# One layer of an RWKV-7 / forgetting-attention trunk: y split inside the first stage, attention with two row blocks under way, transposes of the normed rows one block later, one PSUM pool

## The chip, the cores and the metric

The kernel runs on one core of a Trainium2 chip. A core has five engines with queues of their own: TensorE (PE in the profile, its weight loads PEld) for matmuls and transposes, VectorE (DVE), ScalarE (ACT), GpSimd (POOL), and SyncE (SP), which here only issues DMAs. Matmul results land in PSUM, which has eight banks of 128 partitions by 512 float32 values; everything else lives in SBUF. The metric is the time of one execution on the device in microseconds, and lower is better.

## The reference

One layer, 512 tokens and 16 meta tokens ahead of them (T = 528), width 1024:

```python
u = rmsnorm(h, norm_mix)
proj = u @ w_in                      # 1792 + 1544 + 2048 columns
y_rw = rwkv7_branch(...)             # 8 heads of 64, delta rule, group norm, gate
y_fx = fox_branch(...)               # 8 heads of 64, causal softmax with forgetting
gates = sigmoid(proj[..., C_RW + C_FX:] + b_gate)
merged = gates[..., :1024] * (y_rw @ w_out_rw) + gates[..., 1024:] * (y_fx @ w_out_fx)
h = h + merged @ w_o
z = rmsnorm(h, norm_mlp)
h = h + square(relu(z @ w_up)) @ w_down
return h[:, 16:]
```

## The kernel before

**Precision.** Every large product is made in three passes of float32r matmuls: each operand is split in a high part (a cast on ACT) and a low part (a subtraction on DVE), and high by high, high by low and low by high are added in PSUM. `split` (L269) does this for any tile, `load_h` (L229) for half of a weight block: a DMA into `wraw` (4 buffers), the cast to `whi`, the difference to `wlo`. `load_w` (L239) loads both halves, `passes` (L273) gives the three pairs.

**The front** (L280 to L1133). After a start in an order written by hand, several Python generators ("streams") issue their instructions in turns. `Turns.run` (L164) takes the first stream, by rank, whose next step is ready by a clock that the builder keeps while it writes the program (`Clock`, L62): so the order of TensorE's instructions is fixed when the program is built (L1130), and the other engines and SP are ordered by the framework's scheduler. The streams are
- `recurrent` (L1088): the RWKV heads in four pairs, of which two make a group g. Each pair needs three blocks of the projection (`okk`, `orr`, `ov`); then come `keys`, `rows`, `scores`, the matrix `inverse` of the group, and `chain` (L984), which goes through nine chunks one after the other. `group_norm` writes `y_rw`;
- `fox_features` (L614): for each of four pairs of attention heads the blocks q, k and v, their norms and the transposes of v;
- `attention` (L678): for each pair four row blocks of 128 queries. `scored(i)` makes the logits in PSUM and the softmax in a tile `pe` (2 buffers), `turned(i)` transposes it into `pT`, `mixed` multiplies by v and copies the result to `y_fx` (L752);
- `projections` (L549): 40 blocks of `u @ w_in`, 48 matmuls of 264 columns or 24 of 512 each, taken from a list `jobs` ordered by rank and time of asking (`ask`, L519). RWKV blocks have rank 1, attention blocks 2, the 16 gate blocks 9. A job may name an event (`need`) for which the stream waits before it starts the block. As the lowest stream but one, it fills what the others leave of TensorE.

The gates go to DRAM (`gd`, L589), and their blocks are the filler when nothing else is asked for. PSUM has pool `ps`: tag `pj` with 2 banks, `ch` and `py` with one each for the chain (lent to `projections` while no chain runs), `sm` with 4 for all else.

**After the front** the pools of the front are closed and others opened over their space: `hp` (`hres`, and a tag each for `yhi`/`zhi` and `ylo`/`zlo`), `ps2` for PSUM with 4 banks `po` and 4 `pd`, and `mp`. Then:
- L1150 to L1174: `y_rw` and `y_fx` are split (L1151 to L1153: eight casts and eight subtractions), and for each of 8 blocks m of w_out two groups of 12 matmuls (L1168) are made, weighed with the gates (`gl`, loaded at L1162) and summed to `mhi`/`mlo`;
- L1186 to L1192: two blocks of w_up are loaded ahead through `wraw`; L1195 to L1200: the first half of w_o's columns; L1201 to L1204: its second half is loaded, also through `wraw`, and split;
- L1212 to L1235: per block i of 128 tokens the second half's 24 matmuls (L1217), the addition, the RMS norm (L1220 to L1230), and at once eight transposes of the normed rows (L1233), whose results are split to `zhi`/`zlo`.

**The MLP** (L1240 on) goes in four slices of 8 blocks of w_up: the up products (L1247), squared ReLU, and w_down in seven products per slice (L1365) by a scheme of Strassen's kind, whose right factors are sums of quarters of w_down (`factor_sums`, L1287; raw quarters in `traw`). In the last product of the last slice (`added(0, 1, S4, ...)`, L1418) the two results x[0] and x[1] are added to `hres` (L1382) and stored (L1386).

Of the kernel before, what the change touches and what calls it, by code (L numbers as in the profile page):

```python
# [29 lines left out]
FIRST = (0, 4, 8, 12)  # L30

# [155 lines left out]
def kernel(ctx, tc, ht, x, win, par, cst, gain, lora, wout, wo, wup, wdn, out, dbg=None):  # L187
# [40 lines left out]

    def load_h(src, low, tag, bufs):  # L229
# [5 lines left out]
        A.copy(hi, raw)  # L235
        low.tensor_tensor(lo, raw, hi.bitcast(F32), ALU.subtract)  # L236
        return hi, lo
# [38 lines left out]
    yp = ctx.enter_context(tc.tile_pool(name="yp", bufs=1))  # L276
    gates_d = [dr.tile([128, S], F32, name=f"gd{i}") for i in range(16)]
    quarters = [[wdn[i][256 * c:256 * c + 256] for c in range(8)] for i in range(4)]

    with ExitStack() as st:  # L280
        up = st.enter_context(tc.tile_pool(name="up", bufs=1))
        ps = st.enter_context(tc.tile_pool(name="ps", bufs=2, space=PSUM))
# [33 lines left out]
        fF = rp.tile([8, T], F32, name="fF", tag="Bm", bufs=2)  # L316
        fF_d = dr.tile([8, T], F32, name="fF_d")
        f0 = rp.tile([8, T], F32, name="f0", tag="L0", bufs=2)
        f1 = rp.tile([8, T], F32, name="f1", tag="L1", bufs=2)
# [197 lines left out]
        asked = [0]  # L517

        def ask(rank, blk, begin, parts=((0, HT), (HT, T)), need=None):  # L519

            ev = Event()
            jobs.append((rank, asked[0], blk, begin, parts, ev, need))
            jobs.sort(key=lambda j: j[:2])
            asked[0] += 1
            return ev
# [72 lines left out]

        forgot = Event()
# [13 lines left out]

        def fox_features():  # L614
            for p in range(4):
                b0 = B_PAIR + 6 * p
                if p > 1:
                    yield fox_near[p - 2]

                def ask_normed(blk, parts, name, need=None):  # L620
                    d = {}

                    def begin():
                        c0 = parts[0][0]
                        d["f"] = f = fp.tile([128, T - c0], F32, name=name, bufs=2)
                        d["sq"] = sq = fp.tile([128, T], F32, name="fsq", tag="fsq", bufs=2)

                        def evac(po, sl):
                            d["s"] = act(sq[:, sl], po, AF.Square)
                            A.copy(f[:, sl.start - c0:sl.stop - c0], po)  # L630
                        return evac
                    d["in"] = ask(2, blk, begin, parts, need)
                    return d

                def normed(d, parts, gcol):
                    yield d["in"]
                    f, sq = d["f"], d["sq"]
                    yield lambda: max(ck.ready(sq), banks(len(parts)))
                    pin = None
                    for a0, a1 in parts:  # L640
                        pq = psm("pssq")[:, :a1 - a0]
                        mm(pq, ones_blk, sq[:, a0:a1], start=True, stop=True)
                        pin = pin or pinned(d["s"])
                        after(act(sq[:, a0:a1], pq, AF.Ln, bias=eps, scale=1.0 / 64), pin)
                    c0 = parts[0][0]
                    act(sq[:, c0:], sq[:, c0:], AF.Exp, scale=-0.5)
                    V.scalar_tensor_tensor(f, f, gcol, sq[:, c0:], ALU.mult, ALU.mult)
                    return f

                whole = ((0, HT), (HT, T))  # L650
                dq, dk, d = ask_normed(b0, SEQ, "qa", fox_done[p - 2] if p > 1 else None), ask_normed(b0 + 1, whole, "ka"), {}
                q_done = Event()

                def begin():
                    d["v"] = fp.tile([128, T], F32, name="vf", tag="fsq", bufs=2)
                    return lambda po, sl: A.copy(d["v"][:, sl], po)
                v_in = ask(2, b0 + 2, begin, need=q_done)
                q = yield from normed(dq, SEQ, qg8)
                q_done.done = True
                k = yield from normed(dk, whole, pr[:, C_KG:C_KG + 1])  # L660
                yield v_in
                vf = d["v"]
                yield lambda: max(ck.ready(vf), banks(2))
# [3 lines left out]
                for j in range(4):  # L667
                    nc.tensor.transpose(pv[:, 128 * j:128 * j + 128], vf[:, NM + 128 * j:NM + 128 * j + 128], ident)
                A.copy(vt.rearrange("p a b -> p (a b)"), pv)
                pvm = psm("pvm")  # L670
                nc.tensor.transpose(pvm[:16, :128], vf[:, :NM], ident)
                for e, hs in enumerate(hss):
                    A.copy(vm[32 * e:32 * e + 16, hs], pvm[:16, hs])
                yield forgot
# [3 lines left out]
        def attention():  # L678
            for p in range(4):
# [12 lines left out]
                def scored(i):  # L692
# [11 lines left out]
                    for e in range(2):  # L704
                        pe = fp.tile([128, T], F32, name="pe", bufs=2)
# [35 lines left out]
                def mixed():  # L741
# [52 lines left out]
        class Pair:  # L794
# [70 lines left out]
            def rows(self):  # L865

                kkn, r3, P = v9(self.okk), v9(self.orr), self.P
                self.L = l0, l1 = [rp.tile([128, NCH, 128], F32, name=f"L{e}", bufs=2) for e in range(2)]
# [17 lines left out]
            def scores(self):  # L886
# [3 lines left out]
                self.bkT = bkT = rp.tile([128, NCH, 128], F32, name="bkT", bufs=2)  # L890
                self.Bm = Bm = rp.tile([128, NCH, 128], F32, name="Bm", bufs=2)
# [92 lines left out]
        def chain(g, prs):  # L984
# [21 lines left out]
            for c in range(NCH):  # L1006
# [78 lines left out]
        values_read = [Event() for g in range(2)]  # L1085
        chained = [Event() for g in range(2)]

        def recurrent():  # L1088
# [4 lines left out]
            for g in range(2):  # L1093
                prs = pairs[2 * g:2 * g + 2]
                for j, q in enumerate(prs):
# [14 lines left out]
                    if j == 0:  # L1110
                        yield from prs[1].decay()
                    yield q.v_in
# [6 lines left out]
                if g == 0:  # L1119
                    pairs[2].ask_values(values_read[0])  # L1120
# [5 lines left out]
        turns.add(3, fox_features())  # L1126
        turns.add(8, projections(24 + 16))
# [10 lines left out]
    yhi = hp.tile([128, KB, S], F32R, name="yhi", tag="zhi")  # L1138
    ylo = hp.tile([128, KB, S], F32R, name="ylo", tag="zlo")
    ps = ctx.enter_context(tc.tile_pool(name="ps2", bufs=4, space=PSUM))  # L1140

    def ppo():
        return ps.tile([128, 512], F32, name="po")

    def ppd():
        return ps.tile([128, 512], F32, name="pd")

    with ExitStack() as st:
        mp = st.enter_context(tc.tile_pool(name="mp", bufs=1))
        ahead = [load_w(wout[0])]  # L1150
        for j, src in enumerate((y_rw, y_fx)):  # L1151
            for k in range(4):
                split(yhi[:, 4 * j + k, :], ylo[:, 4 * j + k, :], src[:, k, :])  # L1153
# [3 lines left out]
        for m in range(KB):  # L1157
            w = ahead.pop() if ahead else load_w(wout[m])
            pp = []
            for br in range(2):  # L1160
# [5 lines left out]
                for k in range(4 * br, 4 * br + 4):  # L1166
                    for a, b in passes(wk(w, k), (yhi, ylo)):
                        mm(po, a, b[:, k, :], start=n == 0, stop=n == 11)  # L1168
# [13 lines left out]
        zhi = hp.tile([128, KB, S], F32R, name="zhi", tag="zhi")  # L1182
# [313 lines left out]
```

## Time and profile before

| | us |
|---|---|
| three timed executions | 845.28, 847.02, 847.98 (median 847.02) |
| the profiled execution | 845.82 |
| its span in the trace | 844.1 |
| PE busy | 827.1 (98% of the span) |
| DVE busy | 606.7 (72%) |
| ACT busy | 453.5 (54%) |
| last matmul of the front starts | 415.21 |
| first product of w_out starts (L1168) | 417.17 |
| first up product starts (L1247) | 510.29 |
| last matmul starts | 839.73 |

The granted clock of TensorE is 1.00 in every slice. "Busy" of PE counts from the start of a matmul to its modelled end, and neighbours overlap, so 98% does not say that no time is lost: the distance from one matmul's start to the next one's does.

### The profile page before, as it was taken

The numbers are of one execution on the slowest core, as the hardware profiler recorded it, in microseconds if no ns is written. First come the engines' busy times: TensorE is split into PE (matmuls) and PEld (weight loads), VectorE is DVE, ScalarE is ACT, GpSimd is POOL, SyncE is SP. The second block draws the span as 40 slices with busy tenths as digits, with TensorE's granted clock in tenths as the row PEclk, the third lists the DMA queues.
The fourth block names the chain that finished last, engine by engine and source line by source line (L and its number), as shares of the span: only waits on it lengthen the run. The fifth ranks groups of instructions, "written<-read, shape, count | busy, mean of one in ns | idle before, by whom it ended". The sixth has DMA issues, their size and how long they took to land.

```text
span 844.1 us, 15258 instructions
## 1 busy us (share of the span) xinstructions
PE 827.1 (98%) x5746; PEld 677.1 (80%) x5746; DVE 606.7 (72%) x1208; ACT 453.5 (54%) x934; POOL 112.6 (13%) x121
## 2 busy tenths in 40 slices
PE   8989998999999999999999999999999999999998
PEld 6979886788978767877688779888888888888886
DVE  6797975679799357655556564876687777768688
ACT  7767537765763456544556442664354445544452
POOL 1011000001010000000022002204700550055000
PEclk9999999999999999999999999999999999999999
DMA  7221231101222322233486423642753374345431
GB/s 233 73 94 59 69 97 62 56 27 52 63 64 69 97 79 73 64 92 104 147 270 224 150 75 88 202 149 67 235 150 99 97 239 129 84 138 192 119 90 75
DMA packets 51338, 95.88 MB, mean 114 GB/s; under 512 B 5816, under 2 KB 6968, under 8 KB 51264
## 3 DMA queue, kind: packets, MB, share of 16 engines
q1 hardware_dynamic: 47680, 86.52, 32.8%
q0 software_dynamic: 1280, 4.20, 1.7%
q10 hardware_dynamic: 2304, 4.20, 1.5%
q8 instruction: 45, 0.74, 0.4%
q14 instruction: 29, 0.24, 0.1%
HBM read 88.57 MB, written 6.31 MB: 112 GB/s over the span
## 4 chain that ended last, share of the span: by engine, by line
PE 78%; DVE 9%; ACT 5%; DMA 4%; issue 3%; POOL 1%; SPq 0%; DVEq 0%; ACTq 0%; POOLq 0%
PE pj L575 22%; PE po L1247 21%; PE po L1365 12%; PE pd L1365 5%; DMA gl<-gd 2%; PE pw L951 2%; PE po L1217 2%; PE psc L701 2%; PE pj L390 1%; PE ppt L733 1%; DVE wlo L545 1%; DMA wraw<-in_wup 1%; PE py L749 1%; DVE wlo L236 1%; DMA wraw<-in_wo 1%
## 5 line engine op out<-in xcount | busy, mean ns | idle before, releaser
L575 PE MATMUL pj<-uhi,whi 128*128 128x264 f32 (+1 forms) x480 | 166.2, 346 | 0.0
L575 PE MATMUL pj<-ulo,whi 128*128 128x264 f32 (+1 forms) x480 | 154.0, 321 | 0.0
L575 PE MATMUL pj<-uhi,wlo 128*128 128x264 f32 (+1 forms) x480 | 154.0, 321 | 0.0
L575 PEld LDWEIGHTS pj<-uhi,whi 128*128 128x128 f32 x480 | 90.2, 188 | 14.1 <-issue 5.7
L575 PEld LDWEIGHTS pj<-ulo,whi 128*128 128x128 f32 x480 | 90.4, 188 | 6.9 <-issue 2.1
L575 PEld LDWEIGHTS pj<-uhi,wlo 128*128 128x128 f32 x480 | 90.3, 188 | 7.0
L1247 PE MATMUL po<-zhi,whi 128*128 128x512 f32 (+1 forms) x248 | 94.8, 382 | 0.0
L1247 PE MATMUL po<-zlo,whi 128*128 128x512 f32 (+1 forms) x248 | 94.8, 382 | 0.0
L1247 PE MATMUL po<-zhi,wlo 128*128 128x512 f32 (+1 forms) x248 | 94.8, 382 | 0.0
L236 DVE TENSOR_TENSOR wlo<-wraw,whi 128x512 fp32r<-128x512 f32 x84 | 65.1, 785 | 41.1 <-ACT whi L235 41.1
L235 ACT CAST whi<-wraw 128x512 fp32r<-128x512 f32 x84 | 51.3, 617 | 46.8 <-DMA wraw<-in_wup 25.2
L544 ACT CAST whi<-wraw 128x512 fp32r<-128x512 f32 x78 | 47.8, 618 | 47.8 <-PE pj L575 47.5
L545 DVE TENSOR_TENSOR wlo<-wraw,whi 128x512 fp32r<-128x512 f32 x78 | 53.0, 689 | 24.9 <-ACT whi L544 23.1
L270 ACT CAST whi<-t 128x512 fp32r<-128x512 f32 x64 | 39.9, 624 | 44.5 <-DVE wlo L271 20.6
L271 DVE TENSOR_TENSOR wlo<-t,whi 128x512 fp32r<-128x512 f32 x64 | 49.3, 784 | 18.9 <-ACT whi L270 18.0
L1365 PE MATMUL po<-wlo,fhi 128*128 128x512 f32 x160 | 62.7, 392 | 0.2 <-DVE wlo L271 0.2
L1365 PE MATMUL po<-whi,flo 128*128 128x512 f32 x160 | 62.3, 390 | 0.0
L1365 PE MATMUL po<-whi,fhi 128*128 128x512 f32 x160 | 62.0, 389 | 0.0
L1293 POOL TENSOR_TENSOR t<-traw 128x512 f32<-128x512 f32 x24 | 35.7, 1492 | 153.2 <-DVE wlo L271 134.3
L1247 PEld LDWEIGHTS po<-zhi,wlo 128*128 128x128 f32 x248 | 46.6, 188 | 9.1
L1247 PEld LDWEIGHTS po<-zlo,whi 128*128 128x128 f32 x248 | 46.6, 188 | 9.0
L1247 PEld LDWEIGHTS po<-zhi,whi 128*128 128x128 f32 x248 | 46.6, 188 | 9.0
(316 smaller groups left out, 1733.1 us busy)
## 6 DMA issues: line engine op xcount, KB each, us to landing
wraw<-in_win SPq DMA_DIRECT2D x84, 256.0 KB, 2.6
wraw<-in_wup SPq DMA_DIRECT2D x64, 256.0 KB, 3.3
wraw<-in_wdn SPq DMA_DIRECT2D x48, 256.0 KB, 2.6
traw<-in_wdn SPq DMA_DIRECT2D x48, 256.0 KB, 2.9
gd<-gt ACTq DMA_DIRECT2D x16, 256.0 KB, 2.3
wraw<-in_wout SPq DMA_DIRECT2D x16, 256.0 KB, 3.1
gl<-gd SPq DMA_DIRECT2D x16, 256.0 KB, 3.5
wraw<-in_wo SPq DMA_DIRECT2D x16, 256.0 KB, 3.3
```

Of the source, the lines that this page charges most:

```text
L235: A.copy(hi, raw)
L236: low.tensor_tensor(lo, raw, hi.bitcast(F32), ALU.subtract)
L270: A.copy(hi, x)
L271: V.tensor_tensor(lo, x, hi.bitcast(F32), ALU.subtract)
L544: after(A.copy(hi, raw), last["ACT"])
L545: after(V.tensor_tensor(lo, raw, hi.bitcast(F32), ALU.subtract), last["DVE"])
L575: mm(po, a, b[:, k, a0:a1], start=n == 0, stop=n == 23)
L701: mm(sc, q[hs, 128 * i:128 * i + 128], k[hs, a:b], start=True, stop=True)
L951: mm(ps_[hs, n - b0, :], lhs(n)[hs], rhs(n)[hs], start=True, stop=True)
L1247: mm(po[:, t0:t1], a, b[:, k, t0:t1], start=n == 0, stop=n == 23)
L1293: eng.tensor_tensor(t, sums[c, pair] if c in (T1, T2) else c, d, ALU.add)
L1365: mm(x[i], a[:, k, left, 128 * i:128 * i + 128], c, start=start and k == 0 and n == 0, stop=stop and k == n_pairs - 1 and n == 2)
```

## The change

- A pool `kp` and the PSUM pool `ps` are opened ahead of the front and live to the end. The tags L0, L1, bkT and Bm (two buffers each) of the recurrence move from `rp` to `kp`; `ppo` takes banks of tag `sm`, `ppd` those of `pj`, `ch`, `py` in turn.
- The split of y becomes a stream of the front, `divided`, of rank 4. It writes eight tiles `ys` into the slots of L0, L1, bkT and Bm, once chain 1 has ended; the last attention pair is split straight from PSUM.
- `fox_features` asks for q and k of pair 1 at the beginning, right behind pair 0's blocks, with `need` on pair 0's k and v.
- `attention` issues `scored(i + 1)` ahead of `turned(i)`; the tile `pe` has two tags by parity of the block, with two buffers each.
- The values of pair 2 of the recurrence are asked for in chain 0's last chunk but one, where before they were asked for with `need` on that place.
- The early blocks of w_up and the second half of w_o are loaded into space of `zlo` and `zhi` in place of `wraw`.
- The transposes of block i of the normed rows are called after the norm of block i + 1.
- In the last product, x[1] is made as two results of 256 columns; each is added and stored by itself, the first of the two through ACT's queue.
- The sums of w_down's quarters lie in the slots of `kp`, the raw quarters' loads on SP are kept behind the last `load_h` issued, and the scratch for dynamic DMAs is halved.

The core of the diff (of the class Fox, only what differs from the functions before):

```diff
+SLOTS = ("L0", "L1", "bkT", "Bm")
@@ load_h
-        nc.sync.dma_start(raw, src)
+        asked.append(nc.sync.dma_start(raw, src))
@@
+    kp = ctx.enter_context(tc.tile_pool(name="kp", bufs=1))
+    ps = ctx.enter_context(tc.tile_pool(name="ps", bufs=2, space=PSUM))
+        def two(j, k):
+            ys[4 * j + k] = t = kp.tile([128, 2, S], F32R, name="ys", tag=SLOTS[(4 * j + k) // 2], bufs=2)
+            return t[:, 0, :], t[:, 1, :]
+        def divided():
+            yield chained[1]
+            for k in range(2):
+                split(*two(0, k), y_rw[:, k, :])
+            for k in range(3):
+                yield fox_done[k]
+                split(*two(1, k), y_fx[:, k, :])
+            yield normalised[1][1]
+            for k in range(2, 4):
+                split(*two(0, k), y_rw[:, k, :])
@@ fox_features
+            fox = [Fox(p) for p in range(4)]
+            fox[0].ask()
+            fox[0].ask_values()
+            fox[1].ask(fox[0].k_done, fox[0].v_done)
+            for p, x in enumerate(fox):
                 if p > 1:
                     yield fox_near[p - 2]
+                    x.ask(fox_done[p - 2])
+                if p > 0:
+                    x.ask_values()
...
@@ attention
-                        pe = fp.tile([128, T], F32, name="pe", bufs=2)
+                        pe = fp.tile([128, T if i % 2 else T - 128], F32, name=f"pe{i % 2}", bufs=2)
-                    A.copy(y_fx[:, p, :], py)
+                    if p < 3:
+                        A.copy(y_fx[:, p, :], py)
+                    else:
+                        yield chained[1]
+                        split(*two(1, 3), py)
                 for i in range(4):
+                    if i < 3:
+                        nxt = yield from scored(i + 1)
+                        fox_near[p].done = i == 2
                     yield from turned(i, pes)
-                    if i < 3:
-                        pes = yield from scored(i + 1)
-                        fox_near[p].done = i == 2
+                    pes = nxt
@@ chain, recurrent
                         values_read[g].done = True
+                        if g == 0:
+                            seconds[0].ask_values()
-                    pairs[2].ask_values(values_read[0])
+                    seconds.append(pairs[2])
@@ after the front
-        for j, src in enumerate((y_rw, y_fx)):
-            for k in range(4):
-                split(yhi[:, 4 * j + k, :], ylo[:, 4 * j + k, :], src[:, k, :])
-                    for a, b in passes(wk(w, k), (yhi, ylo)):
-                        mm(po, a, b[:, k, :], start=n == 0, stop=n == 11)
+                    for a, b in passes(wk(w, k), (0, 1)):
+                        mm(po, a, ys[k][:, b, :], start=n == 0, stop=n == 11)
+        raws = [hp.tile([128, KB, S], F32, name=name + "raw", tag=name) for name in ("zhi", "zlo")]
-                raw = wp.tile([128, 512], F32, name="wraw", bufs=4)
+                raw = raws[1][:, 2 * j + x, :]
-            raw = wp.tile([128, 512], F32, name="wraw", bufs=4)
+            raw = raws[0][:, k, :]
...
-                pt = ppd().rearrange("p (b c) -> p b c", c=128)
-                for k in range(4):
-                    nc.tensor.transpose(pt[:, k, :], xt[:, 512 * j + 128 * k:512 * j + 128 * k + 128], ident)
-                A.copy(zhi[:, kk, tk], pt)
-                V.tensor_tensor(zlo[:, kk, tk], pt, zhi[:, kk, tk].bitcast(F32), ALU.subtract)
+            if normed:
+                turned(*normed.pop())
+            normed.append((i, xt))
+        turned(*normed.pop())
@@ MLP
+            if name == "traw" and queue is nc.sync:
+                after(d, asked[-1])
+            return [(0, WHOLE)] + ([(1, WHOLE)] if len(x) == 2 else [(1, cols) for cols in HALVES])
-                x = [ppo() for i in range(2)]
+                x = [ppo() for i in range(2 + end)]
+                    if end:
+                        store(a, b, i, cols, nc.scalar if n == 1 else nc.sync)
@@ kernel
-    nc = bacc.Bacc("TRN2", target_bir_lowering=False, num_devices=1, dynamic_dma_scratch_size=8192)
+    nc = bacc.Bacc("TRN2", target_bir_lowering=False, num_devices=1, dynamic_dma_scratch_size=4096)
```

More of the change, by code (lines that the diff above doesn't have):

```diff
@@ L281 @@
         up = st.enter_context(tc.tile_pool(name="up", bufs=1))
-        ps = st.enter_context(tc.tile_pool(name="ps", bufs=2, space=PSUM))
         def ppj(tag):
@@ L635, in normed @@
[L635 to L663, printed above, removed]
+                    x.ask(fox_done[p - 2])
+                if p > 0:
+                    x.ask_values()
+                q = yield from x.normed(x.dq, SEQ, qg8)
+                x.q_done.done = True
+                k = yield from x.normed(x.dk, x.WHOLE, pr[:, C_KG:C_KG + 1])
@@ L664, in fox_features @@
+                x.k_done.done = True
+                yield x.v_in
+                yield lambda: max(ck.ready(x.v), banks(2))
                 vt = fp.tile([128, 4, 128], F32, name="vt", bufs=2)
```

139 lines of the change are left out of this document (92 added, 47 removed).

## The prediction

> **What bounds the kernel now.** I read the page first, then what PE waited for, then the chain of waits in order of time, then a table by stage.
>
> ```profile
> span 844.1 us, 15258 instructions
> PE 827.1 (98%) x5746; PEld 677.1 (80%) x5746; DVE 606.7 (72%) x1208; ACT 453.5 (54%) x934; POOL 112.6 (13%) x121
> ```
> ```profile
> PE pvt L997 <- ACT gt L588: 2.1, 1, 2.1
> PE psr L898 <- DVE Bm L899: 1.9, 4, 0.8
> PE po L1168 <- ACT yhi L270: 1.6, 1, 1.6
> ...
> PE pd L1233 <- DVE xt L1230: 0.8, 1, 0.8
> ```
> ```profile
> core 0: us, PE busy (x) PEld busy (x) DVE busy (x) ACT busy (x) POOL busy (x), PEclk, DMA share, GB/s
> ...
> 352.00:415.60 63.60, 63.60 (x352) 47.26 (x351) 33.91 (x97) 28.29 (x72) 0.00 (x0) 1.00 0.30 95
> 415.60:418.00 2.40, 0.60 (x3) 0.29 (x2) 1.54 (x3) 2.40 (x5) 0.00 (x0) 1.00 0.38 106
> ...
> 515.00:844.00 329.00, 324.96 (x1484) 270.01 (x1482) 247.19 (x342) 154.46 (x245) 80.36 (x64) 1.00 0.45 138
> ```
>
> TensorE bounds every stage. In the waits' list (total, times, longest) no entry is over 2.1 us, and in the table (length of the stretch, then busy time by engine) only the handover at 415.6 to 418 is mostly empty. The change removes no matmul, so it can gain only what TensorE loses between matmuls: waits, and the switches between its kinds of work. For these I need the steady distance of starts:
>
> ```profile
> 92.30 5.82 PE pj L575 x48
> ...
> 146.75 0.92 PE pj L575 x6
> ...
> 594.22 43.52 PE po L1247 x192
> ```
>
> These are rows of the chain (start, length, what, count). A product of 512 columns takes 43.52 / 192 = 0.227 us, one of 264 columns 5.82 / 48 = 0.121. Six of the latter between other work take 0.92 and not 6 x 0.121 = 0.73: an interruption of the filler costs 0.19.
>
> **Term 1, the handover: -2.2.** The filler's last matmul, the casts of y and the first two products of w_out:
>
> ```profile
> 415.21 0.40 PE L575 MATMUL pj<-uhi,wlo 128*128 128x512 f32 x1
> ...
> 416.51 0.61 ACT L270 CAST yhi<-y_rw 128x512 fp32r<-128x512 f32 x1
> ...
> 417.17 0.49 PE L1168 MATMUL po<-yhi,whi 128*128 128x512 f32 x1 [1.57 <-ACT yhi L270]
> ...
> 417.90 0.50 PE L1168 MATMUL po<-ylo,whi 128*128 128x512 f32 x1 [0.23 <-DVE ylo L271]
> ```
>
> From 415.21 to 417.90 are 2.69 us for two steps worth 0.45, so 2.24 are lost. yhi needs the space that the filler still reads, hence the late cast. In the change the pieces of y lie in other slots and are split earlier, after chain 1; ACT is busy 28.29 and DVE 33.91 of the 63.6 us there, so eight casts of 0.61 and their subtractions fit beside the filler. Only the last attention pair can be late, and its part is wanted after 12 products of the other branch, 2.7 us. Bounds: nothing to -2.24; I take it whole, since PE's other operands, the first weights, are already in.
>
> **Term 2, the weights of w_o: -1.2.**
>
> ```profile
> 477.67 0.62 ACT L270 CAST wohi<-wraw 128x512 fp32r<-128x512 f32 x1 [2.36 <-DMA wraw<-in_wo]
> ...
> ```
> ```profile
> 478.08 0.39 PE L1200 MATMUL po<-whi,mlo 128*128 128x512 f32 x1
> ...
> 480.01 0.40 PE L1200 MATMUL po<-whi,mlo 128*128 128x512 f32 x1
> ```
>
> Three steps take 1.93 us instead of 0.68: 1.25 lost. ACT sits in order behind a cast whose load came late, since both halves of w_o share the four `wraw` buffers. With loads into the space of zlo and zhi that cast's data comes sooner. Bounds 0 to -1.25.
>
> **Term 3, the transposes: -1.2.**
>
> ```profile
> 492.54 0.39 PE L1217 MATMUL po<-wohi,mhi 128*128 128x512 f32 x1
> 493.71 0.66 PE L1233 MATMUL pd<-cs,xt 128*128 128x128 f32 x4 [0.78 <-DVE xt L1230]
> ...
> 495.11 0.39 PE L1217 MATMUL po<-wohi,mhi 128*128 128x512 f32 x1
> ```
> ```profile
> 499.90 0.39 PE L1217 MATMUL po<-wohi,mhi 128*128 128x512 f32 x1
> ...
> 501.64 0.39 PE L1217 MATMUL po<-wohi,mhi 128*128 128x512 f32 x1
> ```
>
> The same work (a product, four transposes, a product, four transposes, a product) takes 2.57 us in block 0 and 1.74 in block 1, so block 0 loses 0.83 to the norm. A block later every row is ready: this goes. The eight transposes then stand together, which saves one interruption per block, at most 4 x 0.19 = 0.76; I take 0.4. Bounds 0 to -1.6. Block 3's transposes still wait for their norm, but behind them lie the first up products, as now.
>
> **Term 4, the tail: +0.1.**
>
> ```profile
> 839.47 1.39 DVE L1382 TENSOR_TENSOR hres<-hres,po 128x512 f32<-128x512 f32 x2 [0.34 <-PE po L1365]
> ...
> 839.73 0.40 PE L1365 MATMUL po<-whi,flo 128*128 128x512 f32 x1
> ```
> ```profile
> L1081 DVE TENSOR_TENSOR y_rw<-yT,pg 128x256 f32<-128x256 f32 x8 | 3.3, 417 | 0.3
> ```
>
> The two last additions already run back to back on DVE, 0.69 each, and the last matmul ends before the second begins. Halving x[1] makes that 0.69 + 2 x 0.42 = 1.53 instead of 1.39, by the nearest row of 256 columns; 12 products become 24 halves, about the same array time. Against it the last store is half as large:
>
> ```profile
> L1386 SPq DMA_DIRECT2D out<-hres x8: 332/332/344, 814.4 to 840.9; - x8
> ...
> DMA to landing us min/median/max: 2.0/2.0/2.0
> ```
>
> Between nothing and half of 2.0 could be saved. I take 0.1 lost, bounds +0.2 and -0.9. [...]
>
> **Term 5, the front's order: -1.5.** Nothing is added or taken from TensorE there. With pair 1 asked for at the beginning its q and k stand where three gate blocks stood, and these gates fill later. `scored(i + 1)` ahead of `turned(i)` gives every attention step more time for its softmax, and pair 1 then runs beside chain 0. Each pair has 11 steps, 44 in all; where a step falls next to one of the chain's, one interruption of 0.19 goes. I take 8 of 44, an estimate: -1.5. From both sides: 20 steps more merged, -3.8; as many split apart, +3.8. One wait can go or stay:
>
> ```profile
> 134.78 0.70 ACT L588 ACTIVATE gt<-pj,pr 128x512 f32<-128x512 f32 x1
> ...
> 135.53 0.41 PE L997 MATMUL pvt<-cs,ov 128*64 128x128 f32 x2 [2.11 <-ACT gt L588]
> ```
>
> Chain 0 wants the bank `py` that a gate block borrowed, and ACT empties it late. Another block may stand there with the same effect, so I count 0, and -2.1 in the range. The later asking for pair 2's values moves a block that no one waits for now. The added `need` can hold only the `projections` stream, and pair 1's blocks stand behind pair 0's in its list anyway, so I cost it at nothing.
>
> The rest costs nothing: raw quarters, kept behind loads already issued, are wanted an up phase later, and from 515 on PE is busy 324.96 of 329 us, with no wait in the list above 0.3. The PSUM tags of `ppo` and `ppd` make again four and four banks.
>
> **The sum**: -2.2 - 1.2 - 1.2 + 0.1 - 1.5 = -6.0 us. The profiled execution took 845.82 (1.7 around its span), so 839.8. It lies 1.2 below the median of the timed runs, 847.02; from the middle of the two, 846.4, I get **840.4**.
>
> **Rivals.**
> *The handover's gain is given back (842.6).* The loads of w_up and w_o, 12 x 256 KB, can now start at 415.
>
> ```profile
> 417.00:455.00 38.00, 37.60 (x165) 30.92 (x166) 25.03 (x40) 24.15 (x43) 7.76 (x6) 1.00 0.78 258
> ```
> ```profile
> 427.32 0.60 ACT L235 CAST whi<-wraw 128x512 fp32r<-128x512 f32 x1
> ```
>
> The DMA engines are busy at 0.78 there, and 3 MB at 258 GB/s are 12 us of their work. The cast at 427.32 is that of block 2's second half, wanted by matmul 60 of the stage, at 417.90 + 59 x 0.227 = 431.3, or 429.1 if the stage starts 2.2 earlier; with its subtraction about 1 us is left. A load later by over 1 us stalls PE. For it: ACT's casts stand in order behind the gates' tanh, which wait for DMAs. Against: SP spreads such loads in time even now. Price: 2.2.
>
> *The front loses what the rest gains (844.9).* More attention beside the chains means more changes of shape on TensorE: 24 more interruptions cost 4.5. [...]
>
> *Slower (849.5 or more): the filler runs out.* The chain shows the last attention pair at
>
> ```profile
> 387.52 0.87 PE psc L701 x4
> ...
> 399.24 1.09 PE psc L701 x8
> ...
> 411.40 1.00 PE py L746 x4
> ```
>
> that is 12 us per row block, nearly all of it filled by gate blocks. If the gates were used up before the last pair's third row block, PE would stand in two such blocks with some 2 us of work in each: up to 20 us. From 8.5 us on, less than half of that, the kernel is slower. Against it: pair 1's blocks push gates back, so three more are left then, not fewer.
>
> *Some edits do nothing (842)*: the scheduler orders all but the front by readiness, so the regrouping and the loads may come out as now; that is inside the forecast's own range.
>
> **Chances.** Forecast (837 to 842.5): 0.56. A front that gains 3 us more (below 837): 0.11. Handover given back: 0.11. Front loses: 0.14. Slower: 0.08. A change of 0.3%, 2.5 us, is about what a measurement of this kernel can tell from none. The first three are faster: 0.78; the fourth counts as the same: 0.14; slower 0.08. The range takes in the front's bounds and the first two rivals, and most of the third: 835.5 to 845.
>
> **What would show it.** Right: the first L1168 starts within 0.3 us of the last filler matmul's turn; no wait of L1200 on ACT; L1233 in groups of eight; the last store no sooner after the last matmul than now; fewer runs of L575 in the front. Wrong: waits at L1168 for `whi`; attention's steps with nothing of L575 between them and PE idle; new waits of the chain's first lines.

## The result, and the profile after

The changed kernel took 841.21 us (median of 4 runs, 840.85 to 841.58) where the kernel before, timed beside it, took 847.50 (4 runs, 845.28 to 848.49): a ratio of 0.9929, 95% interval 0.9908 to 0.9950. The forecast was 840.4. The profiled execution took 840.95, with a span of 839.2, 4.9 less than before; so the sum of the prediction, -6.0 on one profiled execution, came out as -4.9, and several of its parts came out otherwise than forecast.

The page of the changed kernel begins:

```profile
span 839.2 us, 15281 instructions
PE 826.2 (98%) x5758; PEld 679.4 (81%) x5758; DVE 606.9 (72%) x1209; ACT 451.9 (54%) x933; POOL 117.8 (14%) x121
```

TensorE still bounds the kernel, and its busy time hardly moved (827.1 before, 826.2 now). The span fell by 4.9: what went was time between matmuls. Where, is read from the starts of the first matmul of each stage in the timelines (us; the last column is the span):

| | last of the filler | 1st of w_out | 1st of w_o | w_o, 2nd half | 1st up product | span |
|---|---|---|---|---|---|---|
| before | 415.21 | 417.17 | 461.31 | 484.38 | 510.29 | 844.1 |
| changed | 412.92 | 413.15 | 457.03 | 481.13 | 505.49 | 839.2 |
| difference | -2.29 | -4.02 | -4.28 | -3.25 | -4.80 | -4.9 |

By stage: the front -2.29, the handover with the second product -2.2, the rest of w_out +0.2, the first half of w_o **+1.03**, the second half with the transposes -1.55, the MLP and the tail -0.1. Four stages gained; w_out and the first half of w_o gave 1.3 us back. The two ends of that are in the timeline of TensorE in the changed kernel (start, length, line, what, and in brackets the wait in front of it):

```profile
412.92 0.39 PE L580 MATMUL pj<-uhi,wlo 128*128 128x512 f32 x1
413.15 0.62 PE L1213 MATMUL po<-ys,whi 128*128 128x512 f32 x2
...
458.62 0.50 PE L1244 MATMUL po<-whi,mhi 128*128 128x512 f32 x1 [0.75 <-DVE gl L1215]
...
467.62 0.50 PE L1244 MATMUL po<-wlo,mhi 128*128 128x512 f32 x1 [0.76 <-DVE wlo L239]
```

The first product of w_out follows the last of the filler after 0.23 us, the steady distance: the handover is gone. But the first half of w_o, where the change was to take a stall away, has two new ones. The chain of waits in front of the second says what it is (start, length, what):

```profile
459.57 5.57 DMA zhiraw<-in_wo
...
465.16 0.02 ACT wohi L273
...
465.69 0.61 ACT whi L238
466.30 0.53 ACT wohi L273
...
466.89 0.69 DVE wlo L239
```

A raw block of the second half of w_o (`zhiraw`) lands at 465.14, 5.57 us after its issue. ACT stands in order with its cast (`wohi`), and behind that stands the cast of the first half (`whi`) that TensorE needs now; the load of that one had landed at 464.51, 1.2 us before its cast began. It is the old stall of 478 again, with the same cause, sooner. The queue that issues the loads shows why (SP's own rows: start, time from the first issue to the last, what, how many):

```profile
455.19 0.33 SPq L1207 DMA_DIRECT2D gl<-gd  x1
455.57 0.42 SPq L1247 DMA_DIRECT2D zhiraw<-in_wo  x1
456.40 0.33 SPq L235 DMA_DIRECT2D wraw<-in_wo  x1
456.78 0.90 SPq L1247 DMA_DIRECT2D zhiraw<-in_wo  x2
459.20 0.33 SPq L235 DMA_DIRECT2D wraw<-in_wo  x1
459.57 0.91 SPq L1247 DMA_DIRECT2D zhiraw<-in_wo  x2
```

With room of their own, the loads of the second half no longer wait for one of four buffers, so they go out between those of the first half and of the gates (`gl`), over 20 us before anyone wants them.

### The profile page after: what moved, and what is told of

The parts are those of the page before. It is cut to its first block, busy times and chain, and to the rows that moved or that the text cites. A ratio compares the mean times of both kernels' runs of the same rounds, so it can differ in the third digit from the quotient of the medians.

```text
span 839.2 us, 15281 instructions
## 1 busy us (share of the span) xinstructions
PE 826.2 (98%) x5758; PEld 679.4 (81%) x5758; DVE 606.9 (72%) x1209; ACT 451.9 (54%) x933; POOL 117.8 (14%) x121
## 4 chain that ended last, share of the span: by engine, by line
PE 84%; DVE 6%; ACT 4%; DMA 3%; issue 2%; POOL 1%; SPq 0%; DVEq 0%; ACTq 0%; POOLq 0%
PE pj L580 24%; PE po L1302 21%; PE po L1429 12%; PE pd L1429 5%; PE po L1274 3%; PE pw L993 2%; PE psc L738 1%; PE pj L395 1%; DMA gl<-gd 1%; PE py L786 1%; PE ppt L770 1%; PE pch L1059 1%; PE po L1244 1%; PE pd L1244 1%; DVE wlo L550 1%
## 5 line engine op out<-in xcount | busy, mean ns | idle before, releaser
L239 DVE TENSOR_TENSOR wlo<-wraw,whi 128x512 fp32r<-128x512 f32 x84 | 78.6, 947 | 40.2 <-ACT whi L238 40.0
L550 DVE TENSOR_TENSOR wlo<-wraw,whi 128x512 fp32r<-128x512 f32 x78 | 52.7, 685 | 21.8 <-ACT whi L549 19.2
L1429 PE MATMUL po<-wlo,fhi 128*128 128x512 f32 (+1 forms) x164 | 63.4, 387 | 0.1
L1429 PE MATMUL po<-whi,flo 128*128 128x512 f32 (+1 forms) x164 | 62.9, 384 | 0.0
L1429 PE MATMUL po<-whi,fhi 128*128 128x512 f32 (+1 forms) x164 | 62.3, 384 | 0.0
L274 DVE TENSOR_TENSOR wlo<-t,whi 128x512 fp32r<-128x512 f32 x64 | 43.6, 689 | 24.3 <-ACT whi L273 24.1
L1318 ACT CAST fhi<-R 128x768 fp32r<-128x768 f32 (+1 forms) x32 | 30.2, 944 | 46.1 <-DVE R L1325 25.1
```

Of the source, the lines that this page charges most:

```text
L274: V.tensor_tensor(lo, x, hi.bitcast(F32), ALU.subtract)
L550: after(V.tensor_tensor(lo, raw, hi.bitcast(F32), ALU.subtract), last["DVE"])
L1318: A.copy(fhi[:, j, a:b], R[:, a:b])
L1429: mm(x[i][:, cols], a[:, k, left, 128 * rows:128 * rows + 128], c[:, cols], start=start and k == 0 and n == 0, stop=stop and k == n_pairs ...
```

## The experiments

All times are medians of 4 to 8 runs timed beside the kernel before, whose own medians were 846.6 to 847.1 in the sets of runs 1 to 12. Medians less than about 1 us apart can't be told apart where the runs behind them overlap; there the traces are compared. The last column is the stretch from the first product of w_out to the first of the second half of w_o; its 288 products need 288 x 0.227 = 65.4 us.

| | run | us | ratio to before (95%) | 1st of w_out | that stretch |
|---|---|---|---|---|---|
| | before | 847.5 | | 417.17 | 67.2 |
| | changed | 841.21 | 0.9929 (0.9908 to 0.9950) | 413.15 | 68.0 |
| 1 | front undone | 842.63 | 0.9959 (0.9947 to 0.9970) | 417.09 | 65.4 |
| 2 | raws undone | 841.89 | 0.9946 (0.9934 to 0.9958) | 413.25 | 70.1 |
| 3 | raws and handover undone | 841.73 | 0.9951 (0.9936 to 0.9965) | 414.80 | 66.8 |
| 4 | transposes undone | 841.72 | 0.9950 (0.9937 to 0.9962) | 412.69 | 68.1 |
| 5 | x and gain later | 841.87 | 0.9946 (0.9933 to 0.9958) | 412.51 | 70.6 |
| 6 | second half of w_o later | 838.72 | 0.9909 (0.9896 to 0.9923) | 412.73 | 65.8 |
| 7 | 5 and 6 | 838.93 | 0.9906 (0.9891 to 0.9921) | 413.14 | 67.1 |
| 8 | the kernel before, again | 846.01 | 0.9997 (0.9986 to 1.0009) | 416.61 | 67.5 |
| 9 | 6, handover undone | 841.04 | 0.9924 (0.9904 to 0.9943) | 415.18 | 66.4 |
| 10 | 6, attention's order undone | 835.95 | 0.9863 (0.9845 to 0.9882) | 410.35 | 66.4 |
| 11 | 6, early asking undone | 842.08 | 0.9938 (0.9920 to 0.9955) | 413.36 | 68.9 |
| 12 | 6, tail undone | 839.37 | 0.9902 (0.9883 to 0.9921) | 413.26 | 66.1 |

(In run 1 one product of w_out starts at 413.35, between steps of attention; 417.09 is the second.)

### Run 1: the front as before

```diff
-            fox[1].ask(fox[0].k_done, fox[0].v_done)
+                if p == 1:
+                    x.ask()
-                    if i < 3:
-                        nxt = yield from scored(i + 1)
...
-                    yield from turned(i, pes)
-                    pes = nxt
+                    yield from turned(i, pes)
+                    if i < 3:
+                        pes = yield from scored(i + 1)
```

> The changed kernel with attention as before: pair 1's q and k asked for behind pair 0, and `turned(i)` ahead of `scored(i + 1)`. Only the asking for pair 2's values stays changed. Theory (the order of the front ends it 2.3 us sooner, 412.92 against 415.21, by fewer interruptions of the filler and by the wait of pvt that is gone): the last filler matmul starts at 415 +- 0.5, the filler has over 100 runs where the changed kernel has 87, and the time is 841.2 + 2.3 = 843.5. Rival (it is the later asking for pair 2's values that moved the gate block out of chain 0's way): the wait of pvt stays gone and only the interruptions come back, 842.2 or less.

Measured: 842.63. The longest wait of the kernel before, of `pvt` on a gate's evacuation, is back in the list (total, times, longest):

```profile
PE pvt L1039 <- ACT gt L593: 2.1, 1, 2.1
```

The filler has 95 runs (stretches of its matmuls without others between) up to its end, not the over 100 of the theory, against 88 in the changed kernel. But the front ends in a way that neither theory named (TensorE's timeline):

```profile
410.76 0.39 PE L580 MATMUL pj<-uhi,wlo 128*128 128x512 f32 x1
410.99 0.27 PE L769 MATMUL ppm<-cs,pe 128*16 128x128 f32 x1
...
413.35 0.50 PE L1213 MATMUL po<-ys,whi 128*128 128x512 f32 x1
413.79 1.07 PE L784 MATMUL py<-pTm,vm 16*64 16x512 f32 x2
414.78 2.38 PE L787 MATMUL py<-pT,vt 128*64 128x512 f32 x16
417.09 0.50 PE L1213 MATMUL po<-ys,whi 128*128 128x512 f32 x1
```

The filler runs out at 410.76, and the last attention pair stands nearly alone until 417. So the order of the front is worth 3.7 to 3.9 us at the start of w_out (417.09 against 413.15). That the filler runs out isn't what costs them: TensorE is busy 6.21 of the 6.33 us from 410.76 on. About half of the 3.7 are waits (from 23 us to the end of the front they add up to 6.8 us, in the changed kernel to 4.9, the wait of `pvt` among them); the rest is spread over the front. Only 1.4 reach the total: with the later start the first half of w_o has no stall at all.

### Runs 2 and 3: the raw weights, and the handover with them

Run 2 loads through `wraw` again (`raw = wp.tile([128, 512], F32, name="wraw", bufs=4)` in both places). Run 3 does that, drops `divided`, and splits y behind the front into the space of `zhi` and `zlo`, as before.

> The changed kernel with the early blocks of w_up and the second half of w_o loaded through the four `wraw` buffers, as before. Theory (the loads into the space of zhi and zlo have no brake: 3 MB more are under way before 465 us, and gate and weight loads land late, which makes the two new stalls of 0.9 and 1.0 us in the first half of w_o): the stalls at 457 and 466 go, the old one of 1.25 us in front of the last steps of that half comes back, and the time is 841.2 - 1.9 + 1.2 = 840.5. Rival 1 (the prediction: the old stall comes back and nothing goes): 842.4. Rival 2 (the stalls come from the sooner start of the stage as such): the two stalls stay and the old one is back too, 842.4 as well, but with three stalls in the trace.

> The changed kernel with y split behind the front, into the space of zhi and zlo, and with all raw weights loaded through `wraw`, as before. Theory (the handover is worth 2.2 us and little of it is given back): 2.2 us above the run in which only the raws are undone, so 843 to 844, with PE waiting at the first product of w_out for yhi. Rival (handover's gain given back by loads that land late in the first half of w_o): the stalls of 0.9 and 1.0 us there shrink by as much as the handover takes, and the time is within 0.7 us of that run's.

Run 2: 841.89, from 840.38 to 843.19. Of the three cases none holds whole, though its one run at full clock took 840.38, near the theory's 840.5. The two new stalls go, as the theory had it; the old one comes back, larger, and costs more than its own length (timeline of run 2, then stretches of it, where the columns are the busy times of TensorE, its loads, DVE, ACT and POOL, the granted clock, the DMA engines' share and GB/s):

```profile
474.41 0.39 PE L1243 MATMUL po<-whi,mlo 128*128 128x512 f32 x1
476.31 0.50 PE L1243 MATMUL po<-whi,mhi 128*128 128x512 f32 x1 [1.51 <-ACT whi L238]
477.11 0.50 PE L1243 MATMUL po<-wlo,mhi 128*128 128x512 f32 x1 [0.30 <-DVE wlo L239]
```
```profile
477.00:478.00 1.00, 0.89 (x4) 0.75 (x5) 0.76 (x3) 0.89 (x2) 0.00 (x0) 1.00 0.43 121
478.00:479.00 1.00, 1.00 (x4) 0.80 (x3) 0.63 (x1) 0.00 (x0) 0.00 (x0) 0.50 0.89 334
...
481.00:482.00 1.00, 1.00 (x5) 0.80 (x4) 0.69 (x1) 0.41 (x1) 0.00 (x0) 0.79 0.62 184
```

Behind the wait TensorE is granted half its clock from 478 to about 481.4. Run 3 starts w_out 1.55 us later than run 2 and is no slower (841.73): its stretch to the second half is 66.8 us where run 2 needs 70.1, of which the half clock is 1.6. By the medians and these two traces the theory is out and the rival holds: as the loads stand here, a later handover only takes the stall out of w_o. At full clock it may be otherwise: run 2's only such run took 840.38, run 3's three 841.31 to 842.62, too few to settle it. The second half starts at 481.13 in the changed kernel, 481.60 in run 3, 482.52 in run 1, although w_out starts 4 us apart.

### Run 4: the transposes at once

The body of `turned` stands again inside the loop over j, right behind each half's norm.

> The changed kernel with each block's normed rows transposed right after their norm, as before. Theory (the norm of the first block made TensorE wait 0.8 us and the transposes in two groups of four cost one interruption more per block): PE waits for xt again, the second half of w_o is 1.2 to 1.6 us longer, and the time is 842.4 to 842.8. Rival (with the loads landing otherwise the norm is no longer late): within 0.5 us of 841.2.

Measured: 841.72, 0.5 above the changed kernel, within what the runs spread. The trace is clearer. The chain of waits shows the transposes of the changed kernel in groups of eight, and those of run 4 in fours with a product between:

```profile
492.18 0.87 PE pd L1264 x8
493.05 5.46 PE po L1274 x24
498.51 0.87 PE pd L1264 x8
```
```profile
495.89 0.60 PE pd L1290 x4
496.49 0.24 PE po L1274
496.73 0.44 PE pd L1290 x4
```

From the second half of w_o to the first up product it takes 25.16 us (480.75 to 505.91), the changed kernel 24.36, the kernel before 25.91. No wait for `xt` shows. So the regrouping is worth 0.8, more than the 0.4 assumed, and the norm's wait of 0.8 went with the other parts of the change; which of them took it away isn't shown.

### Runs 5, 6 and 7: which loads are in the way

```diff
5 -        nc.sync.dma_start(gB, gain.to_broadcast([128, 1024]))
5 +        after(nc.sync.dma_start(gB, gain.to_broadcast([128, 1024])), gls[-1])
5 -            nc.sync.dma_start(hres[:, i, :], x[128 * i:128 * i + 128, :])
5 +            after(nc.sync.dma_start(hres[:, i, :], x[128 * i:128 * i + 128, :]), gls[-1])
6 -            nc.sync.dma_start(raw, wo[1, k // 2][:, 512 * (k % 2):512 * (k % 2) + 512])
6 +            after(nc.sync.dma_start(raw, wo[1, k // 2][:, 512 * (k % 2):512 * (k % 2) + 512]), asked[-1])
```

`gls[-1]` is the last load of a gate, `asked[-1]` at that place the last load of w_o's first half; `after` only sets the order on SP's queue. Run 7 has both.

> The changed kernel with the five loads of x and gain (2.5 MB, wanted from 481 us on) held behind the last load of the gates on SP's queue. Theory (from 413 us on the DMA engines are the limit, 0.85 busy up to 457, so loads that no one needs yet push back the gates and the first half of w_o, and that is what the two new stalls of 0.9 and 1.0 us are): the stall on the gates at 457 goes, the one at 467 shrinks or goes, and the time is 839.2 to 840.3. Rival 1 (the gates' loads are late because each has only two buffers, not because of the traffic): both stalls stay, 841.2. Rival 2 (the loads of x then come too late for the additions behind the first half): the second half of w_o waits at its first additions, 842 or more.

> The changed kernel with the raw second half of w_o held on SP's queue behind the last load of its first half. Theory (the eight loads of 256 KB into the space of zhi stand between those of the first half, and ACT stands in order behind a cast whose load has not landed): the stall at 467 (1.0 us with its gap) goes, the one on the gates at 457 may stay, and the time is 840.2 to 840.7. Rival 1 (the traffic as a whole is the limit, so the order of these loads is nothing): 841.2. Rival 2 (held back, they are late for the second half, as in the kernel before): a stall near 479 to 482 of over 1 us, and 842 or more.

> Both of the former together. Theory: both stalls go, w_out and the first half of w_o take 65.5 us where the changed kernel takes 68.0, and the time is 839.0 to 839.6. Rival (11 MB are wanted between 413 and 481 whatever their order, so one stall only moves to the second half): 840.5 or more.

Run 5: 841.87. The theory falls: a wait on a gate moves into w_out (0.5), and one of 1.7 for `whi` appears at 467, again followed by a granted clock of 0.50 (the mean of this trace is 0.998). The five loads now stood right ahead of the first half's weights, and three of these took 7.6 to 7.9 us from issue to landing. In run 5 and run 7 the longest waits between 405 and 515 were

```profile
PE po L1245 <- ACT whi L238: 1.7, 1, 1.7
```
```profile
PE po L1214 <- DVE gl L1216: 1.5, 1, 1.5
```

Run 6: **838.72**, better than its theory, since both stalls went, and no run of it is as long as any of the changed kernel's (838.33 to 840.43 against 840.85 to 841.58). SP and TensorE in run 6 read

```profile
453.59 0.33 SPq L1207 DMA_DIRECT2D gl<-gd  x1
454.79 6.93 SPq L235 DMA_DIRECT2D wraw<-in_wo  x4
461.77 4.11 SPq L1247 DMA_DIRECT2D zhiraw<-in_wo  x8
```
```profile
PE po L1244 <- DVE wlo L239: 0.2, 1, 0.2
```

The last gate's load goes out 1.6 us sooner (453.59 for 455.19), the eight raw blocks follow the first half's, and of the waits between 405 and 515 one of 0.2 is left. The DMA engines are about as busy (the last two numbers are their share and GB/s):

```profile
413.00:457.00 44.00, 44.00 (x196) 36.43 (x195) 26.04 (x39) 24.69 (x42) 10.06 (x7) 1.00 0.80 271
457.00:481.00 24.00, 23.81 (x106) 19.38 (x104) 16.92 (x31) 15.64 (x30) 1.60 (x1) 1.00 0.59 191
```

In the changed kernel the same stretches show 0.85 and 0.52. So it isn't the amount of traffic but its order: loads that aren't wanted yet ahead of those that are, on one queue, and casts in that order on ACT. Run 7: 838.93, as run 6; holding x and gain back too gives nothing. Its time is about what its theory said, its stretch isn't: the wait of 1.5 us on a gate stands in w_out, and the stretch is 67.1 us, not 65.5.

### Run 8: the kernel before, once more

> The kernel before, for another trace of it: of its 11 runs on this chip nine had a mean granted clock of 0.997 or 0.998 and took 846.3 to 847.8, two had 1.000 and 0.998 and took 845.3 to 845.5, while the profile shown of it had 1.000. Theory (the stall of 2.24 us at the handover is sometimes followed by some microseconds at half the clock, as the stall of 1.9 us at 474 is in the run with the raws undone, where the clock is 0.50 from 478 to 481): the trace shows a stretch at about 0.5 behind 417 or behind another of the kernel's longest waits, and the time is 846.3 to 847.8. Rival (the clock is a little lower all over): no stretch stands out.

Measured: a median of 846.01, and 845.33 in the profiled execution, under the theory's 846.3 to 847.8 but with the stretch that it wanted (timeline, then the clock):

```profile
414.64 0.40 PE L575 MATMUL pj<-uhi,wlo 128*128 128x512 f32 x1
416.61 0.51 PE L1168 MATMUL po<-yhi,whi 128*128 128x512 f32 x1 [1.57 <-ACT yhi L270]
417.34 0.56 PE L1168 MATMUL po<-ylo,whi 128*128 128x512 f32 x1 [0.22 <-DVE ylo L271]
...
420.68 0.58 PE L1168 MATMUL po<-yhi,whi 128*128 128x512 f32 x1
421.10 0.40 PE L1168 MATMUL po<-ylo,whi 128*128 128x512 f32 x1
```
```profile
418.00:419.00 1.00, 1.00 (x4) 0.71 (x4) 1.00 (x2) 1.00 (x3) 0.00 (x0) 0.50 1.03 399
...
421.00:422.00 1.00, 1.00 (x5) 0.77 (x5) 0.49 (x1) 0.47 (x1) 0.00 (x0) 0.96 0.51 168
```

The same wait as in the first trace of this kernel is followed here by eight products 0.43 us apart (421.10 less 420.68) and not 0.227: 1.6 us, and w_out takes 45.8 us where it took 44.1. At the end of w_o's first half next to nothing of it is left (second half at 484.15, in the first trace 484.38, where the front ended 0.6 later), since the stall of 478 is gone in turn. Of the 43 timed runs of this kernel beside these experiments, this one's own among them, the six with a mean clock of 1.000 took 845.07 to 845.53; the nineteen of 0.998, this trace's value, took 845.02 to 847.84; the two of 0.999 took 846.04 and 846.36, those of 0.996 and 0.997 846.4 to 848.5, and one of 0.994 took 850.95. The changed kernel's four runs had 0.999 or 1.000. The medians of this kernel are thus 1.3 to 2.2 us above its runs at full clock (846.6 to 847.5 against about 845.3). That the long wait brings this difference too, and the change takes it away with the wait, is likely but not shown: none of the runs of 846 us or more has a trace, and the one stretch that was traced cost the total nothing. The two profiled executions of the kernels before and changed, both at 1.000, differ by 4.9.

### Runs 9 to 12: the parts again, with the loads in order

> The run with the second half of w_o held back (838.7) with one thing undone: the eight casts of y stand on ACT behind the last gate's evacuation, so behind the filler. Theory (the handover is worth the 2.2 us of the prediction, and only the disordered loads of w_o took it back): PE waits some 2 us for ys at the first product of w_out, no other stall gets shorter, and the time is 840.9. Rival 1 (the first half of w_o ends when its weights are in, whatever came before): 839.2 or less, with the first half of w_o ending at 478 to 479 as without the edit. Rival 2 (the long wait also brings the half clock, as in the second trace of the kernel before, where 410 to 430 lost 1.6 us so): 842.5, with a granted clock under 0.95 behind 415.

Run 9 sets the casts of y behind the last gate's evacuation on ACT (`after(A.copy(hi, src[:, k, :]), gated[-1])`). Measured: 841.04, the theory's 840.9:

```profile
413.22 0.39 PE L580 MATMUL pj<-uhi,wlo 128*128 128x512 f32 x1
415.18 0.50 PE L1215 MATMUL po<-ys,whi 128*128 128x512 f32 x1 [1.57 <-ACT ys L1199]
415.91 0.50 PE L1215 MATMUL po<-ys,whi 128*128 128x512 f32 x1 [0.23 <-DVE ys L1200]
```

From the filler's last matmul to the second product are 2.69 us, to the hundredth as in the kernel before, and the total is 2.3 above run 6. (In the traces the spans differ by 3.0: 2.2 at the handover, 0.7 since the front of this trace ended later.) The handover is worth the 2.2 of the prediction, once nothing behind it takes it back.

> The run with the second half of w_o held back (838.7) with `turned(i)` ahead of `scored(i + 1)` again; pair 1 is still asked for at the beginning. Theory (the early asking is what moves the gates back and fills the end of the front, and the order only merges some steps): the first product of w_out starts 0.5 to 1.5 us later than 412.7, the time is 839.2 to 840.2. Rival (the order is the larger part, since a row block's softmax is uncovered without it): 2 us or more later, 840.7 or more.

> The run with the second half of w_o held back (838.7) with pair 1's q and k asked for behind pair 0, as before; `scored(i + 1)` still stands ahead of `turned(i)`. Theory (with both parts undone the filler ended at 410.8 and attention at 417, 3.7 us later than in the changed kernel; the early asking is the larger part, since it leaves gate blocks for the end): 2 to 3.7 us later at the first products of w_out, with attention behind the last filler matmul, and 840.7 to 842.4. Rival (the order is the larger part): under 1 us later, 839.7 or less.

Run 10 has the edit of run 1's second part alone, run 11 that of its first. **Run 10: 835.95.** Both theories had the wrong sign: `scored(i + 1)` ahead of `turned(i)` costs 2.8 us here. The front ends 2.4 sooner (410.35 against 412.73). Counted from one matmul's start to the next one's, attention takes 1.0 less, its features and the filler 0.5 more each, and the recurrence's own products ahead of the chains 2.6 less; its two largest groups, in run 6 and then in run 10 (busy and mean ns; behind the second bar the idle time before them and what ended it):

```profile
L940 PE MATMUL psr<-L,BK 64*64 64x128 f32 x288 | 13.0, 280 | 2.0 <-DVE Bm L941 1.7 <-DVE L L943 0.3
L869 PE MATMUL pup<-lhi,lw 64*128 64x264 f32 x32 | 5.9, 326 | 1.4 <-ACT sg L258 0.8 <-DVE Bm L941 0.5
```
```profile
L939 PE MATMUL psr<-L,BK 64*64 64x128 f32 x288 | 11.9, 279 | 1.6 <-DVE Bm L940 1.3 <-DVE L L942 0.3
L868 PE MATMUL pup<-lhi,lw 64*128 64x264 f32 x32 | 5.2, 326 | 0.5 <-DVE Bm L940 0.5
```

The wait for ACT's `sg` (0.8) is gone, and one for `Bm` is shorter by 0.4; the rest is the same products standing closer together. What makes them do so isn't settled: it was read from two traces only. Fewer interruptions of the filler it is not: the filler has 97 runs here and 88 in run 6.

Run 11: 842.08, in the theory's range but not by its mechanism. The front ends only 0.6 later; the rest is in the stretch behind it, where the order of the loads came out otherwise again (its two longest waits between 405 and 515):

```profile
PE po L1245 <- DVE wlo L239: 1.3, 2, 0.8
PE po L1214 <- DVE gl L1216: 0.5, 1, 0.5
```

Also the 2.1 us of `pvt` are back, as in run 1, and they are in none of the runs that ask early: it is the early asking that removes them. Taken with run 1, the two parts of the front don't add: without early asking, `scored` first saves the end of the front 3.7 us (413.36 against 417.09), with it the same order costs 2.4. And early asking saves 6.7 us with the old order (417.09 against 410.35), 0.6 with the new one.

> The run with the second half of w_o held back (838.7) with x[1] in one piece in the last product, and its store as one. Theory (the prediction's term: one more addition and twelve more matmuls cost about what half a store saves): within 0.3 us of 838.7, the last store issued 0.1 us sooner after the last matmul but 128 KB longer. Rival (the halved store saves up to half of the 2.0 us to landing): 839.2 to 839.6.

Run 12 makes x[1] as one result. Measured: 839.37 (838.56 to 840.08), against 838.33 to 840.43 in run 6: not to be told apart by the times. From the first up product to the end of the span it is 333.9 us with one piece, 333.7 with two. But the one piece here is stored through ACT's queue; in the kernel before, where SP stores it, the same stretch is 333.8 and 333.7 in its two traces. The tail is worth 0 to 0.2.

## Why the prediction held

The total was right to 0.8 us, and part of that is luck: against the profiled executions w_o came out 2.2 worse than its term, the front 0.8 and the transposes and the tail some 0.5 better, and the base was set 1.1 too low. Of its five terms the handover and the tail held, the transposes and the front came near by another way than the one given, and the weights of w_o were wrong in sign.

- **The handover, -2.2**: right in mechanism and size (-2.2 in the profile, 2.3 in run 9).
- **The weights of w_o, -1.2**: wrong in sign, +1.0. The step that failed is "with loads into the space of zlo and zhi that cast's data comes sooner". The casts of the second half did come sooner (the first at 453.2, before at 473.65), and with them the order that had made the stall: ACT again stood behind a cast whose load was under way, in front of one that was wanted. These loads, without a brake, didn't only land sooner; on SP's queue they also went out ahead of others (at 455.57 and 456.78, the first half's at 456.40 and 459.20). Run 6, which changes only the order on SP's queue, brings the time down by 2.5, about what this term promised and lost together.
- **Rival "the handover's gain is given back"** had the right place in view, the loads behind 415, and the wrong instructions: not `whi` of w_out's block 2 but the gates and the first half of w_o. In the changed kernel 1.3 of 2.2 was given back; in run 2, beside run 3, all of it.
- **The transposes, -1.2**: the sum was right (-1.55), its split not: run 4 puts 0.8 on the regrouping, taken at 0.4, and the norm's wait, 0.8, is gone in run 4 too, without the edit that was to remove it.
- **The tail, +0.1**: 0 to -0.2, within the bounds. The additions were put too high: the three took 1.35 us, not 1.53. The halved store itself saved nothing: in the changed kernel the stores of 256 columns took 2.04 and 2.10 us from issue to landing, those of 512 columns 2.0.
- **The front, -1.5**: -2.3, but not by the step given. The filler was to lose 8 interruptions at 0.19; it lost 19 (107 runs to 88), and 2.5 us by the distances of the starts, 0.13 each. The wait of `pvt`, counted at nothing, went as well: 2.1, while the rest of the front took 2.3 more, attention above all (1.6). Nor does the number of interruptions say where the front ends: with 88, 97 and 104 of these runs of the filler in runs 6, 10 and 11, w_out starts at 412.73, 410.35 and 413.36. And "`scored(i + 1)` ahead of `turned(i)` gives every attention step more time" was counted as a gain: beside the early asking it is a loss of 2.4 (run 10).
- **Rival "the filler runs out"** was priced as the way to a slower kernel and given 0.08. The changed kernel doesn't meet it; run 1 does, at 410.76, but TensorE doesn't stand there: it idles 0.12 us up to 417.09. (The rival's sum is off: its 849.5 lies 9.1 above the forecast, not 8.5.)
- **The base**: the profiled execution of the kernel before had the full clock throughout, while most of its timed runs do not (run 8). The middle of the two was taken as the base, 846.4, and the median was 847.5, 1.1 more. The sum promised 1.1 more than the profiled executions show. So the fall between the medians, 6.3, looks like the sum, 6.0, though the terms by themselves gave 4.9.

## What to carry to other kernels

Give a transfer room of its own only together with a place in the order: here, on SP's queue and among ACT's casts, what wasn't wanted yet stood ahead of what was, and the one line that put the loads in order took 2.5 us off (run 6). Measure a saved wait at the end of the next stretch that is bound by loads, not where it was: here more than half of the 2.2 us saved at 413 was gone at 481 until the loads behind were put in order. And undo the parts of a scheduling change one by one: the best kernel of these runs, 835.95 us (0.9863 of before, 0.9845 to 0.9882), is the change with one of its parts taken back and one line added.

## What was not expected of the hardware

In three traces a wait of TensorE cost more than its length. After about 2.2 us lost within 3 (1.74 and 0.50 at the handover of run 8, 1.67 and 0.57 in run 2) the granted clock was 0.50 for about 3.4 us (417.7 to 421.1 and 478.0 to 481.4), in which products of 512 columns took 0.427 us and not 0.227: 1.6 us more. Run 5 shows a third such stretch, behind its wait of 1.7 for `whi`; the mean clock of its trace is 0.998, as in run 8.

The length of the wait doesn't tell when this happens. In the first trace of the kernel before and in run 9 as much was lost at the same handover (1.73 and 0.50 in both), and the clock behind it was 1.00, with products 0.227 us apart. What sets these cases apart is not shown.
